# A transformer trunk in split fp32: the two matmuls of every wide block in one fixed order, the last block of a sum included

## The chip, the cores and the metric

One core of a Trainium2 chip. The metric is device time in microseconds (us) of one execution, the median of the runs; lower is better. TensorE (PE in the profile, its weight loads PEld) multiplies into PSUM, VectorE (DVE) and ScalarE (ACT) work on SBUF and PSUM, GpSimd (POOL) does little here, and SyncE (SP) issues the DMAs.

## The reference

Two layers on 256 latent tokens (and, in layer 0, on 256 context tokens that feed keys and values) of width 1024. Each layer has three sub-layers: SwiGLU, a mixer, SwiGLU, each behind an RMSNorm that is shifted and scaled per channel by a vector `m` worked out from the conditioning:

```python
def swiglu(h, w13, w2):
    a, b = jnp.split(h @ w13, 2, axis=-1)
    return (jax.nn.silu(a) * b) @ w2                 # 1024 -> 2*2816 -> 1024

def ffn_sublayer(h, m, g, w13, w2, base):
    hn = modulate(rms_norm(h, g), m[:, :, base], m[:, :, base + 1])
    return h + 0.5 * m[:, :, base + 2] * swiglu(hn, w13, w2)

for i in range(2):
    x = ffn_sublayer(x, ...)                         # the context too for i = 0
    x = x + m[5] * mixer_i(modulate(rms_norm(x)))    # i = 0: attention | pooling; i = 1: gated conv
    x = ffn_sublayer(x, ...)
return rms_norm(x, final_g)
```

All of it is fp32 with random weights.

## The kernel before

Activations lie transposed: channels on the 128 partitions, the 256 tokens along the free dimension. Each fp32 operand of a product is split in two parts in a narrower format, hi and lo, and a product is the sum of hi·hi, hi·lo and lo·hi. `mm3` does the three as three matmuls. Where an activation's two parts lie side by side as 512 columns, `mm2` needs two: the weights' hi part against all 512 columns (hi and lo at once, into columns 0 to 511 of a PSUM bank), and the weights' lo part against the 256 hi columns (into columns 0 to 255). This is a wide block; a sum is 8 blocks long over the 1024 channels, or 22 blocks long over the 2816 hidden units, all into one bank. An evacuation then adds the two halves of the bank: `joined` (ACT copies the upper half, DVE adds the lower) or `residual` (DVE adds the lower half, then the upper, to the residual stream `xl_all`).

Wide sums stand in five kinds of places, 148 sums in all: in three feed-forward sub-layers the hidden units f = 6 to 21 (`pf`, two sums each, 96), and the way back (`pz`, 8 sums of 22 blocks each, 24); the two output projections of the mixers (`pwo`, 8 and 8); the conv projections j = 4 to 7 (`pc` two sums, `pb` one, 12). The rest, from 0 to about 490 us and the first hidden units of each sub-layer, goes through `mm3` and a native fp32 form.

Weights come through `Stream`: SP loads 1 MB (`raw`, 3 buffers) with two chunks of 8 blocks in it; per chunk ACT casts the hi part (`whi`, line 102, 4 buffers) and DVE subtracts for the lo part (`wlo`, line 103, 4 buffers). A cast can start once PE has read the chunk four places earlier for the last time. DVE also works out the modulation vectors `m` (line 203, tile `jk`), doled out by `mod_credit`.

PSUM has three double banks (`pair`) and two single ones (`single`). `pf` and `pc` use pairs; `pz`, `pb` and most of `pwo` use singles, so sum d + 2 of these waits for the evacuation of sum d. In the output projections the first sums are begun without the block whose activation comes last (`early`), and that block is done afterwards (`rest`).

The order on each engine is fixed when the program is built: a scheduler with a cost of its own for each instruction places them, with priority for evacuations that feed the next sub-layer. So an edit in one place can reorder instructions elsewhere.

Of the kernel before, what the change touches and what calls it, by code (L numbers as in the profile page):

```python
# [119 lines left out]
def hybrid_trunk_kernel(ctx: ExitStack, tc: tile.TileContext, xc, cols_d, modw, wst, poolw_d,  # L120
                        rpb, notok_d, rcnt_d, out):
    nc = tc.nc
# [133 lines left out]
    def mm2(out, w, x, first, last):  # L256

        (wh, wl), both = w, x.rearrange("p a b -> p (a b)")
        if not last:
            nc.tensor.matmul(out, wh, both, start=first, stop=False)  # L260
        nc.tensor.matmul(out[:, 0:256], wl, x[:, 0, :], start=False, stop=False)  # L261
        if last:
            nc.tensor.matmul(out, wh, both, start=False, stop=True)  # L263

    class Rstd:

# [135 lines left out]
    def wide(pt, w, act):  # L402
        for k in range(KD):
            mm2(pt, (w[0][:, k, :], w[1][:, k, :]), act.op[:, k], k == 0, k == KD - 1)
# [493 lines left out]
    class OutProj:  # L898
# [7 lines left out]
        def block(self, d, k, first, last):  # L906
            assert (d, k) == self.order.pop(0)
            mm2(self.pts[d], W.block(), self.x[:, k], first, last)
# [27 lines left out]
    def ffn(act, l, s, gp, nxt_of, rate1, rate2):  # L936
# [44 lines left out]
        for d in range(KD):  # L981
            pt = single(f"pz{l}{s}{d}")
            for f in range(NF):
                if W.at_chunk():
                    mod_credit(rate2)
                mm2(pt, W.block(), g2[f], f == 0, f == NF - 1)
            residual(pt, d, l, s)
            nxt.feed(d)
# [214 lines left out]
```

## Time and profile before

| | |
|---|---|
| median of 3 runs | 1185.64 us (1185.47 to 1185.81) |
| profiled execution, its own time | 1185.92 us |
| its span, first to last instruction | 1184.1 us |
| mean granted TensorE clock | 0.990 of full speed |
| matmuls that end a wide sum (line 263) | 148 |

A group's row reads: line, engine, operation, tile written <- tiles read, shapes, count. In a row of the timeline the first number is the start in us from the span's start, the second the duration of the stretch; a matmul's duration includes its way through the array, and the next one starts before it ends, so the distance from start to start tells the pace. Equal rows that follow each other are merged ("x2").

### The profile page before, as it was taken

The numbers are of one execution on the slowest core, as the hardware profiler recorded it, in microseconds if no ns is written. First come the engines' busy times: TensorE is split into PE (matmuls) and PEld (weight loads), VectorE is DVE, ScalarE is ACT, GpSimd is POOL, SyncE is SP. The second block draws the span as 40 slices with busy tenths as digits, with TensorE's granted clock in tenths as the row PEclk, the third lists the DMA queues.
The fourth block names the chain that finished last, engine by engine and source line by source line (L and its number), as shares of the span: only waits on it lengthen the run. The fifth ranks groups of instructions, "written<-read, shape, count | busy, mean of one in ns | idle before, by whom it ended". The sixth has DMA issues, their size and how long they took to land.

```text
span 1184.1 us, 16775 instructions
## 1 busy us (share of the span) xinstructions
PE 1154.5 (97%) x6570; PEld 990.4 (84%) x6570; DVE 928.4 (78%) x1486; ACT 573.9 (48%) x890; POOL 21.1 (2%) x23
## 2 busy tenths in 40 slices
PE   4999999999999999999999999999999999999997
PEld 2568888888888987889888889888889989988886
DVE  8977686577788586788898998788998888766663
ACT  4353221223234445567556447555546656655642
POOL 2000000000000040000000000000000000000000
PEclk7999999999999999999999999999999999999998
DMA  7764455467676753245677985677895465555551
GB/s 274 255 221 156 179 191 185 143 217 275 241 272 238 230 136 90 76 165 187 242 264 271 342 316 205 221 271 260 314 336 188 149 213 174 183 181 191 198 179 36
DMA packets 45791, 250.54 MB, mean 212 GB/s; under 512 B 12944, under 2 KB 13328, under 8 KB 17552
## 3 DMA queue, kind: packets, MB, share of 16 engines
q1 hardware_dynamic: 45712, 249.48, 60.4%
q8 instruction: 51, 0.84, 0.3%
q14 instruction: 28, 0.23, 0.1%
HBM read 248.41 MB, written 1.05 MB: 211 GB/s over the span
## 4 chain that ended last, share of the span: by engine, by line
PE 93%; DVE 2%; DMA 1%; SPq 1%; ACT 1%; issue 1%; DVEq 0%; ACTq 0%
PE pf L260 13%; PE pz L260 10%; PE pf L261 8%; PE pa L253 6%; PE pa L254 6%; PE pa L252 6%; PE pz L261 5%; PE p L562 4%; PE py L253 3%; PE py L254 3%; PE py L252 3%; PE pf L253 3%; PE pf L252 3%; PE pf L254 3%; PE pwo L260 2%; PE pf L263 2%
## 5 line engine op out<-in xcount | busy, mean ns | idle before, releaser
L102 ACT CAST whi<-raw 128x1024 fp32r<-128x1024 f32 x312 | 327.8, 1051 | 394.2 <-PE pa L253 114.1
L103 DVE TENSOR_TENSOR wlo<-raw,whi 128x1024 fp32r<-128x1024 f32 x312 | 382.0, 1225 | 150.6 <-ACT whi L102 149.9
L260 PE MATMUL pf<-al,whi 128*128 128x512 f32 x672 | 241.0, 397 | 0.0
L203 DVE CUSTOM_DVE_ANT_0 jk<-mr,cvec,cols 128x1024 bf16<-128x1024 f32 x184 | 236.5, 1285 | 1.6
L261 PE MATMUL pf<-al,wlo 128*128 128x256 f32 x768 | 199.9, 281 | 0.0
L260 PE MATMUL pz<-g,whi 128*128 128x512 f32 x504 | 178.6, 398 | 0.0
L261 PEld LDWEIGHTS pf<-al,wlo 128*128 128x128 f32 x768 | 145.0, 189 | 8.9
L260 PEld LDWEIGHTS pf<-al,whi 128*128 128x128 f32 x672 | 126.4, 188 | 26.2
L261 PE MATMUL pz<-g,wlo 128*128 128x256 f32 x528 | 144.3, 281 | 0.0
L260 PEld LDWEIGHTS pz<-g,whi 128*128 128x128 f32 x504 | 94.7, 188 | 22.1
L252 PE MATMUL pa<-xh,whi 128*128 128x512 f32 x288 | 112.0, 389 | 0.0
L253 PE MATMUL pa<-xl,whi 128*128 128x512 f32 x288 | 112.0, 389 | 0.0
L254 PE MATMUL pa<-xh,wlo 128*128 128x512 f32 x288 | 112.0, 389 | 0.0
L261 PEld LDWEIGHTS pz<-g,wlo 128*128 128x128 f32 x528 | 99.7, 189 | 2.3
L253 PE MATMUL pf<-ah,whi 128*128 128x258 f32 x288 | 81.6, 283 | 0.0
L252 PE MATMUL pf<-ah,whi 128*128 128x258 f32 x288 | 80.9, 281 | 0.0
L254 PE MATMUL pf<-ah,wlo 128*128 128x258 f32 x288 | 80.8, 281 | 0.0
L252 PE MATMUL py<-gh,whi 128*128 128x512 f32 x176 | 68.5, 389 | 0.0
L253 PE MATMUL py<-gl,whi 128*128 128x512 f32 x176 | 68.5, 389 | 0.0
L254 PE MATMUL py<-gh,wlo 128*128 128x512 f32 x176 | 68.5, 389 | 0.0
L619 ACT COPY tf<-pf 128x512 f32<-128x512 f32 x48 | 28.2, 587 | 73.4 <-PE pf L263 73.4
L252 PEld LDWEIGHTS pa<-xh,whi 128*128 128x128 f32 x288 | 54.1, 188 | 11.3
(257 smaller groups left out, 1915.7 us busy)
## 6 DMA issues: line engine op xcount, KB each, us to landing
raw<-in_wst SPq DMA_DIRECT2D x156, 1024.0 KB, 5.0
mr<-in_modw SPq DMA_DIRECT2D x64, 1024.0 KB, 5.0
mr<-in_modw SPq DMA_DIRECT2D x16, 512.0 KB, 5.0
raw<-in_wst SPq DMA_DIRECT2D x8, 512.0 KB, 6.5
bias<-in_rpb SPq DMA_DIRECT2D x32, 64.0 KB, 5.8
xl_all<-in_xc SPq DMA_DIRECT2D x2, 512.0 KB, 6.7
xc_all<-in_xc SPq DMA_DIRECT2D x2, 512.0 KB, 8.1
out<-done SPq DMA_DIRECT2D x3, 256.0 KB, 2.6
```

The costliest lines, as they stand in the source:

```text
L102: nc.scalar.copy(hi, src)
L103: self.last = nc.vector.tensor_tensor(lo, src, hi.bitcast(F32), ALU.subtract).ins
L203: nc.vector.tensor_tensor_reduce(out=junk, in0=raw[:, h, :], in1=cvec[:, q, :], scale=1.0, scalar=cols[:, b : b + 1], op0=ALU.mult, op1=AL ...
L252: nc.tensor.matmul(out, wh, xh, start=first, stop=False)
L253: nc.tensor.matmul(out, wh, xl, start=False, stop=False)
L254: nc.tensor.matmul(out, wl, xh, start=False, stop=last)
L260: nc.tensor.matmul(out, wh, both, start=first, stop=False)
L261: nc.tensor.matmul(out[:, 0:256], wl, x[:, 0, :], start=False, stop=False)
L263: nc.tensor.matmul(out, wh, both, start=False, stop=True)
L562: nc.tensor.matmul(pts[j], wf[:, j * P : j * P + P], f32, start=first, stop=last)
L619: nc.scalar.copy(t, pt[:, :, 256:512])
```

## The change

In `mm2` the last block of a sum had its two matmuls in the other order: first the 256-column one, then the 512-column one, which closed the sum. Now every block has the 512-column matmul first and the 256-column one second, which closes the sum:

```diff
     def mm2(out, w, x, first, last):
 
         (wh, wl), both = w, x.rearrange("p a b -> p (a b)")
-        if not last:
-            nc.tensor.matmul(out, wh, both, start=first, stop=False)
-        nc.tensor.matmul(out[:, 0:256], wl, x[:, 0, :], start=False, stop=False)
-        if last:
-            nc.tensor.matmul(out, wh, both, start=False, stop=True)
+        nc.tensor.matmul(out, wh, both, start=first, stop=False)
+        nc.tensor.matmul(out[:, 0:256], wl, x[:, 0, :], start=False, stop=last)
```

Lines behind it move up by three: the 512-column matmul is line 259 in the kernel after, the 256-column one line 260, and line 619 becomes 616. Both kernels have 6450 matmuls of the same shapes. The upper half of the bank is final one matmul earlier than the lower now, so the built program lets the two be signalled apart: 729 instructions of PE signal to other engines instead of 623.

The end of a sum on PE, in a feed-forward sub-layer (`pf_5344` is the pair of f = 18, `pf_5395` of f = 19; `whi`, `wlo` with a number are a chunk of weights). Before:

```order
L260 MATMUL pf_5344<-al_4346,whi_5288 128x512
L261 MATMUL pf_5344<-al_4346,wlo_5289 128x256 x2
L263 MATMUL pf_5344<-al_4346,whi_5288 128x512
L260 MATMUL pf_5395<-al_4346,whi_5308 128x512
L261 MATMUL pf_5395<-al_4346,wlo_5309 128x256
L260 MATMUL pf_5395<-al_4346,whi_5308 128x512
```

And after:

```order
L259 MATMUL pf_5344<-al_4346,whi_5288 128x512
L260 MATMUL pf_5344<-al_4346,wlo_5289 128x256
L259 MATMUL pf_5344<-al_4346,whi_5288 128x512
L260 MATMUL pf_5344<-al_4346,wlo_5289 128x256
L259 MATMUL pf_5395<-al_4346,whi_5308 128x512
L260 MATMUL pf_5395<-al_4346,wlo_5309 128x256
```

The pair of 256-column matmuls and the pair of 512-column ones around a sum's end are gone; the two sizes alternate throughout.

ACT at the end of the first phase of layer 0's second feed-forward, f = 21 (`tf_5490` is the copy of `pf_5446`'s upper half, `sl_5489` its SiLU, `g_21_4204` the hidden unit that the last block of each `pz` sum reads). Before:

```order
L949 CAST g_20_4203<-sl_5438 128x256
L619 COPY tf_5490<-pf_5446 128x512
L102 CAST whi_5512<-raw_5345 128x1024
L947 ACTIVATE sl_5489<-tf_5490 128x256
L102 CAST whi_5539<-raw_5396 128x1024
L949 CAST g_21_4204<-sl_5489 128x256
L160 ACT_TABLE_LOAD
L160 ACTIVATE warm<-warm 128x1
L102 CAST whi_5561<-raw_5396 128x1024
```

And after:

```order
L946 CAST g_20_4203<-sl_5438 128x256
L102 CAST whi_5512<-raw_5345 128x1024
L616 COPY tf_5490<-pf_5446 128x512
L102 CAST whi_5539<-raw_5396 128x1024
L944 ACTIVATE sl_5489<-tf_5490 128x256
L102 CAST whi_5561<-raw_5396 128x1024
L946 CAST g_21_4204<-sl_5489 128x256
```

Each step of the evacuation now stands behind one more cast of weights. The same exchange of a cast and a copy stands at most f of the feed-forward sub-layers; on DVE the joins and the splits are exchanged likewise, and at this f two more `jk` and one more split stand ahead of `g_21_4204`.

PE at the end of the first `pz` sum of that sub-layer (`pz_5509`; `pz_5582` is the second). Before:

```order
L260 MATMUL pz_5509<-g_20_4203,whi_5469 128x512
L261 MATMUL pz_5509<-g_20_4203,wlo_5470 128x256
L261 MATMUL pz_5509<-g_21_4204,wlo_5470 128x256
L263 MATMUL pz_5509<-g_21_4204,whi_5469 128x512
L260 MATMUL pz_5582<-g_0_4183,whi_5469 128x512
```

And after:

```order
L259 MATMUL pz_5509<-g_20_4203,whi_5469 128x512
L260 MATMUL pz_5509<-g_20_4203,wlo_5470 128x256
L259 MATMUL pz_5582<-g_0_4183,whi_5469 128x512
L260 MATMUL pz_5582<-g_0_4183,wlo_5470 128x256
L259 MATMUL pz_5582<-g_1_4184,whi_5469 128x512
L260 MATMUL pz_5582<-g_1_4184,wlo_5470 128x256
L259 MATMUL pz_5582<-g_2_4185,whi_5512 128x512
L260 MATMUL pz_5582<-g_2_4185,wlo_5513 128x256
L259 MATMUL pz_5582<-g_3_4186,whi_5512 128x512
L259 MATMUL pz_5509<-g_21_4204,whi_5469 128x512
L260 MATMUL pz_5509<-g_21_4204,wlo_5470 128x256
```

Seven matmuls of the second sum now stand ahead of the first sum's last block. Two more places on PE are reordered: behind the even output projection nine matmuls of f = 1 move behind the rest of f = 0, and in the odd output projection five matmuls of the third sum (`pwo_8803`) move ahead of the second (`pwo_8784`), while on DVE the join `tb_8752`, which frees that second sum's bank, moves behind four instructions. On SP three loads change places.

## The prediction

> **What bounds the kernel now.** I read the page's busy times first, then the chain that ended last, then the busy time by stretches, and last the pace of single matmuls around the end of a sum, since the change sits there. The page's busy times and, from its section on the chain, the shares by engine:
>
> ```profile
> PE 1154.5 (97%) x6570; PEld 990.4 (84%) x6570; DVE 928.4 (78%) x1486; ACT 573.9 (48%) x890; POOL 21.1 (2%) x23
> PE 93%; DVE 2%; DMA 1%; SPq 1%; ACT 1%; issue 1%; DVEq 0%; ACTq 0%
> ```
>
> PE is busy 97% of the span and is 93% of the chain. These are averages, so the stretches in which wide sums run come next (busy us of PE, PEld, DVE, ACT, POOL, then the granted clock, the DMA share and GB/s):
>
> ```profile
> 527.00:644.50 117.50, 117.50 (x743) 105.77 (x742) 99.72 (x151) 73.67 (x116) 0.00 (x0) 1.00 0.67 236
> 644.50:709.00 64.50, 64.50 (x374) 56.35 (x373) 60.86 (x99) 32.20 (x42) 0.00 (x0) 1.00 0.88 320
> 963.00:990.00 27.00, 25.82 (x154) 22.46 (x153) 24.47 (x45) 16.69 (x27) 0.00 (x0) 1.00 0.47 167
> ```
>
> In layer 0's second feed-forward (527 to 644.5 the `pf` sums, 644.5 to 709 the `pz` sums) PE has no idle time at all and its clock is at full; DVE is at 99.72 of 117.50 and 60.86 of 64.50, close behind. So in these stretches only two things change the time: PE's own pace at the end of a sum, and something that DVE or ACT delivers late enough to stop PE. In the third stretch, around the odd output projection, PE is idle for 1.18 of 27.00 us; that wait is looked at below.
>
> **The pace at the end of a sum.** PE's rows at the end of one `pf` sum (start, duration; starts tell the pace):
>
> ```profile
> 600.09 0.40 PE L260 MATMUL pf<-al,whi 128*128 128x512 f32 x1
> ...
> 601.50 0.40 PE L260 MATMUL pf<-al,whi 128*128 128x512 f32 x1
> 601.74 0.40 PE L261 MATMUL pf<-al,wlo 128*128 128x256 f32 x2
> 601.98 0.40 PE L263 MATMUL pf<-al,whi 128*128 128x512 f32 x1
> 602.21 0.40 PE L260 MATMUL pf<-al,whi 128*128 128x512 f32 x1
> 602.45 0.28 PE L261 MATMUL pf<-al,wlo 128*128 128x256 f32 x1
> ```
>
> From 600.09 to 601.50 lie four alternating pairs of a 512- and a 256-column matmul: 1.41 us, .3525 a pair. Within a pair the 512 takes .24 (601.50 to 601.74). The two 256s at the boundary take 601.98 − 601.74 = .24, .12 each; the closing 512 takes 602.21 − 601.98 = .23, although it signals the evacuation, and the next sum's 512 takes .24. The two pairs across the boundary, 601.50 to 602.21, take .71 against 2 × .3525 = .705 inside. The same in a `pz` sum of 22 blocks:
>
> ```profile
> 644.51 0.40 PE L260 MATMUL pz<-g,whi 128*128 128x512 f32 x1
> ...
> 651.57 0.40 PE L260 MATMUL pz<-g,whi 128*128 128x512 f32 x1
> 651.80 0.40 PE L261 MATMUL pz<-g,wlo 128*128 128x256 f32 x2
> 652.04 0.40 PE L263 MATMUL pz<-g,whi 128*128 128x512 f32 x1
> 652.27 0.40 PE L260 MATMUL pz<-g,whi 128*128 128x512 f32 x1
> ```
>
> Twenty pairs from 644.51 to 651.57 are 7.06 us, .353 a pair; the two at the end, 651.57 to 652.27, are .70 against .706. So the order 512, 256, 256, 512 costs what 512, 256, 512, 256 costs, to about ±.01 us, which is the rounding of the rows: +.005 in one place, −.006 in the other.
>
> **The change part by part.**
>
> 1. *The exchange itself.* Nothing is removed or added on PE: 6450 matmuls of the same shapes. At each of 148 sums' ends two neighbours of equal size become two alternating pairs. By the rows above the gain is +.005 or −.006, and I take 0. The ends are ±.01 × 148 = ±1.5 us.
>
> 2. *The weight load that now follows a 256-column matmul.* At a boundary the next sum's first load ran beside a 512-column matmul (.23); now it runs beside a 256-column one (.12). That first load may also have to wait, for its chunk of weights or for its bank. The nearest row is the start of a chunk inside a sum, the ninth block of `pz`, whose load waits on ACT's cast and stands behind a 256. First PE, then the load:
>
> ```profile
> 647.21 0.28 PE L261 MATMUL pz<-g,wlo 128*128 128x256 f32 x1
> 647.33 0.40 PE L260 MATMUL pz<-g,whi 128*128 128x512 f32 x1
> ```
>
> ```profile
> 647.22 0.19 PEld L260 LDWEIGHTS pz<-g,whi 128*128 128x128 f32 x1
> ```
>
> The load begins with the 256 at 647.22 and lasts .19, yet the 512 starts .12 after the 256. So .12 of cover is enough, and I price this at 0. From below it is 0 (a load that is hidden already can't gain); the upper end, .19 − .12 = .07 a sum, is the first rival.
>
> 3. *Signals.* 106 more PE instructions signal. The closing 512, which signals today, takes .23, the plain one .24: 0, at most ±.01 × 106 = ±1.1 us, not in addition to the ±1.5, since it lies in the same boundary rows.
>
> 4. *The evacuation.* The upper half of the bank is final one matmul earlier and the lower half closes the sum. Time from a pair's start to the bank's end: before .12 + .40 = .52 (256 starts, 512 starts .12 later and lasts .40); now .24 + .28 = .52. So `joined`'s second step on DVE and the first step of `residual`, both of which read the lower half, start when they did. Only ACT's copy of the upper half may start earlier, by about .12 (.52 against .40). From the waits:
>
> ```profile
> ACT tf L619 <- PE pf L263: 73.4, 48, 1.8
> PE pwo L260 <- DVE xl_all L603: 2.4, 3, 1.1
> ```
>
> ACT waits for PE at 48 `pf` sums, 73.4 us in all: it has time to spare, and starting earlier hands nothing to PE, which waits for none of it. What covers this 0 is that the `g` tiles are read a whole phase later. The second row is PE's own wait, for `residual` to free the bank in the output projections; it hangs on the closing matmul and so stays. There the last block of each sum stands alone:
>
> ```profile
> 970.86 0.27 PE L261 MATMUL pwo<-y,wlo 128*128 128x256 f32 x1
> 970.98 0.40 PE L263 MATMUL pwo<-y,whi 128*128 128x512 f32 x1
> 972.49 0.47 PE L260 MATMUL pwo<-y,whi 128*128 128x512 f32 x1 [1.12 <-DVE xl_all L603]
> ```
>
> After it the 512 will start at about 970.86, the 256 at 971.10 and end at 971.38, as the 512 does now (970.98 + .40). The gap of 1.5 us to 972.49 remains: 0.
>
> 5. *Instructions that the scheduler moved.* Here a delivery can come late. The tightest is `g_21` at the end of layer 0's second feed-forward. DVE's and ACT's rows of before:
>
> ```profile
> 644.45 1.28 DVE L203 CUSTOM_DVE_ANT_0 jk<-mr,cvec,cols 128x1024 bf16<-128x1024 f32 x1
> 645.66 0.69 DVE L620 TENSOR_TENSOR tf<-pf,tf 128x512 f32<-128x512 f32 x1
> 646.26 1.28 DVE L203 CUSTOM_DVE_ANT_0 jk<-mr,cvec,cols 128x1024 bf16<-128x1024 f32 x1
> 647.46 0.42 DVE L948 TENSOR_TENSOR sl<-tf,sl 128x256 f32<-128x256 f32 x1
> 647.87 1.23 DVE L103 TENSOR_TENSOR wlo<-raw,whi 128x1024 fp32r<-128x1024 f32 x1
> 649.00 0.43 DVE L950 TENSOR_TENSOR g<-sl,g 128x256 fp32r<-128x256 f32 x1
> ```
>
> ```profile
> 648.37 0.40 ACT L949 CAST g<-sl 128x256 fp32r<-128x256 f32 x1
> 648.78 1.28 ACT L160 ACT_TABLE_LOAD   x1
> 650.29 1.05 ACT L102 CAST whi<-raw 128x1024 fp32r<-128x1024 f32 x1
> ```
>
> DVE now has two more `jk` (1.20 each, start to start) and one more split (1.13) ahead of `g_21`: 649.00 + 3.53 = 652.53, done by 652.96. ACT casts the hi part behind `whi_5561`, which starts no later than 650.29: 650.29 + 1.05 + .40 = 651.74, earlier than DVE. PE read `g_21` first at 651.80 + .12 = 651.92; seven matmuls now stand ahead of that, four 512s and three 256s, 4 × .235 + 3 × .12 = 1.30, so it is needed at 653.22. It is ready .26 early by the sum of durations; DVE's splits also wait for ACT's casts, which the sum leaves out, so I put the stall at 0 to .2 us.
>
> The odd output projection is the second place. `tb` frees the bank of the second sum:
>
> ```profile
> 963.35 0.42 DVE L620 TENSOR_TENSOR tb<-pb,tb 128x256 f32<-128x256 f32 x1
> 963.69 0.42 DVE L1013 TENSOR_TENSOR zpad<-tc 128x256 f32<-128x256 f32 x1
> ...
> 965.54 1.01 DVE L1016 SCALAR_TENSOR_TENSOR y<-zpad,cols,y 128x256 f32<-128x256 f32 x2
> ```
>
> ```profile
> 965.21 0.40 PE L260 MATMUL pwo<-y,whi 128*128 128x512 f32 x1
> ```
>
> Moved behind `zpad`, `y`, one split and the first of the two scalar-tensor operations, `tb` starts (965.54 − 963.69) + .52 = 2.37 later, at 965.72, and is done at 966.14. PE's first matmul of `pwo_8784` was at 965.21 and now stands behind three 512s and two 256s, .945: 966.15. A tie, 0 to .1 us. The third place, the nine `pf` matmuls that are exchanged behind the even projection, I give the bounds of the first, 0 to .2. Elsewhere a cast has changed places with a copy, on engines that DVE's 99.72 of 117.50 and ACT's 73.67 show to have room. The loads that change places on SP I price at 0: the DMA share is .67 there, and PE waited for nothing. Together 0 to .5, and I take .2.
>
> **The sum.** The profiled execution's own time is 1185.92 us (span 1184.1). 1185.92 + 0 (boundaries) + 0 (loads) + 0 (signals) + 0 (evacuation) + .2 (moved instructions) = 1186.1. The profiled execution stands .28 above the median of the runs, 1185.64, so against that median it is 1185.8.
>
> **The rivals.**
>
> *Slower, the load comes into the open.* If the next sum's first load can't begin until late in the last matmul, because it waits for a bank or a chunk, a 256 of .12 hides less of its .19 than a 512 of .23 did: up to .07 × 148 = 10.4 us, 1196. It decides from 2.4 / 148 = .016 us a sum. For it: each boundary does carry waits. Against it: the chunk start at 647.33, with a wait and the same cover, keeps the pace of .12. Chance .04.
>
> *Slower, the signals cost.* Were each of the 106 further signals to hold PE by what separates two rows, .01 us, it would be 1.1 us: 1186.9, still inside the bound of no change; to count, a signal would have to cost 2.4 / 106 = .023 us. The closing 512's .23 against .24 of one that doesn't signal speaks against any. Chance .04. The Trainium skill, "TensorE: Matmul & The Clock Gate", section "The cost: per-tile semaphore tail", speaks for this rival: increments on completion serialize, each adding about 26.3 ns to the tail of a group of tiles. By that figure the sum would be an estimated 106 × .0263 = 2.8 us more, 1188.6. The trace of before doesn't show it: the signalling matmul isn't followed by a longer step.
>
> *Slower, a moved delivery is late.* If at one of the three places a delivery slips by a whole split and `jk` (1.13 + 1.20), the stall is about 2.3 us, 1188.1. For it: DVE is at 60.86 of 64.50 us where `g_21` is made. Against it: the .26 left by the sum of durations. Chance .02.
>
> *Faster, a projection's wait goes.* If the earlier upper half let the bank free sooner, PE's 2.4 us of waits for `residual` at the projections would go: 1185.8 − 2.4 = 1183.4, or, with .005 less at each of the 96 `pf` boundaries, 1182.9. For it: the upper half is final sooner. Against it: `residual` reads the lower half first, which closes last. Chance .05.
>
> **How the numbers follow.** A measurement of this kernel can tell about 0.2%, 2.4 us, from no change; the three runs lie within .34 us. The likeliest is no change, .85, at 1185.8; faster .05; slower .04 + .04 + .02 = .10. The range comes from the bounds of the likeliest: ±1.5 for the boundaries, to which the moved instructions can add .3 above what I took; with the spread of the runs (.1) below, 1184.2 to 1187.7. The rivals outside it hold under .2.
>
> **What would show it right or wrong.** Right: PE's starts alternate by .24 and .12 straight through a sum's end, two `pf` sums are 16 × .3525 = 5.64 us apart, PE is busy in the whole of both stretches of the second feed-forward, and the wait at the odd projection is still about 1.1 us on `residual`. Wrong: a step of more than .13 behind each closing 256 (load or signals), idle time of PE on `g` in the first or second `pz` sum above .2 us or on `tb` at the odd projection, or a wait at the projections that is gone.

## The result, and the profile after

The kernel after takes 1180.59 us (median of 5 runs, 1179.86 to 1181.26) against 1185.71 for the kernel before in the same measurement: a ratio of .9948, 95% interval .9936 to .9959 (the two medians alone give .9957). Measured again later beside other kernels it took 1180.56 against 1185.79, .9956 (.9944 to .9969). The change makes the kernel faster by about 5.1 us, where no change was forecast (1184.2 to 1187.7).

The page of the kernel after, busy times and shares of the chain:

```profile
PE 1147.9 (97%) x6570; PEld 989.1 (84%) x6570; DVE 927.6 (79%) x1486; ACT 573.6 (49%) x890; POOL 21.1 (2%) x23
PE 93%; DVE 2%; DMA 1%; SPq 1%; ACT 1%; issue 1%; DVEq 0%; ACTq 0%
```

PE bounds it as before, with as many instructions; DVE and ACT do the same work, and PE's busy time fell by 6.6 us. So PE does the same matmuls faster. The clock doesn't explain it: its mean was .990 in the profiled execution before and .997 in the one after, but two runs of the kernel after at .990 took 1180.59 and 1179.86 us, and one of the kernel before at .997 took 1185.60. The stretches by busy time (the second one ends with the `pz` sums here, the last one is shifted with the kernel's progress):

```profile
527.00:644.50 117.50, 117.50 (x755) 107.00 (x755) 99.59 (x151) 74.06 (x117) 0.00 (x0) 1.00 0.69 243
644.50:705.70 61.20, 61.20 (x354) 53.47 (x353) 58.35 (x96) 30.97 (x41) 0.00 (x0) 1.00 0.91 328
959.50:986.50 27.00, 25.40 (x152) 22.03 (x151) 24.16 (x45) 16.71 (x27) 0.00 (x0) 1.00 0.49 170
```

In the first stretch PE has no idle time in either kernel, at a clock of 1.00 in both, but gets through 755 matmuls in 117.50 us instead of 743; at its end both kernels stand at the same place, the start of `pz` (644.51 and 644.57). The columns that one reads first, busy share and clock, show nothing; the count behind the "x" does. PE's rows around the first sum's end, with one far behind:

```profile
557.90 0.39 PE L259 MATMUL pf<-al,whi 128*128 128x512 f32 x1
...
558.25 0.39 PE L259 MATMUL pf<-al,whi 128*128 128x512 f32 x1
558.48 0.28 PE L260 MATMUL pf<-al,wlo 128*128 128x256 f32 x1
558.59 0.39 PE L259 MATMUL pf<-al,whi 128*128 128x512 f32 x1
558.82 0.28 PE L260 MATMUL pf<-al,wlo 128*128 128x256 f32 x1
558.94 0.39 PE L259 MATMUL pf<-al,whi 128*128 128x512 f32 x1
...
644.22 0.39 PE L259 MATMUL pf<-al,whi 128*128 128x512 f32 x1
```

The matmul at 558.48 ends a sum and signals; the next sum's starts .11 later. From 557.90 to 644.22 lie 249 pairs, .3467 us each. Before, a pair inside a sum took .3525. The gain lies in every pair, and not at the sums' ends. A group's mean shows it too, 397 ns for the 512-column matmuls of `pf` before and 391 after (first row before, second after):

```profile
L260 PE MATMUL pf<-al,whi 128*128 128x512 f32 x672 | 241.0, 397 | 0.0
```

```profile
L259 PE MATMUL pf<-al,whi 128*128 128x512 f32 x768 | 266.4, 391 | 0.0
```

Where the time went, by the start of the first matmul of each stage in the profiled executions (us; the stages left out differ by .13 at most between before and after). "Once", "pf only" and "twice, k = 6" are experiments of the next section:

| stage | before | after | after, again | once | pf only | twice, k = 6 |
|---|---|---|---|---|---|---|
| up to the even projection | 490.9 | 492.3 | 490.6 | 491.2 | 490.4 | 490.5 |
| even projection, first hidden units | 63.4 | 63.6 | 63.7 | 63.6 | 63.7 | 63.5 |
| `pf`, 256 pairs | 90.20 | 88.76 | 88.76 | 90.40 | 90.20 | 90.40 |
| `pz`, 176 pairs | 62.04 | 61.14 | 62.14 | 61.18 | 62.17 | 61.18 |
| layer 1: `pf` | 90.20 | 88.76 | 88.76 | 90.40 | 90.20 | 90.40 |
| `pz` | 62.04 | 61.01 | 61.01 | 62.19 | 62.17 | 62.19 |
| conv sums | 33.94 | 34.05 | 34.05 | 34.06 | 33.97 | 34.05 |
| odd projection | 18.25 | 18.65 | 18.79 | 18.79 | 18.14 | 18.79 |
| last: `pf` | 90.20 | 88.76 | 88.76 | 90.40 | 90.20 | 90.40 |
| `pz` | 62.04 | 61.01 | 61.01 | 62.19 | 62.18 | 62.19 |
| span | 1184.1 | 1178.7 | 1178.8 | 1185.3 | 1184.4 | 1184.7 |

From before to after, three `pf` stages give 3 x 1.44 = 4.32 us and three `pz` stages .90 + 1.03 + 1.03 = 2.96, together 7.28. In the second profile of the kernel after the first `pz` stage took 62.14, and the same sum is 6.28. The odd projection gives .40 back, the conv sums .11. The first row differs by 1.3 us and holds the same program in all kernels; over the profiles it lies between 490.3 and 492.3, and that is chance. 256 pairs in 88.76 us are .3467 each; 90.20 is .3523, and 90.40 .3531.

### The profile page after: what moved, and what is told of

Same layout as the page of the kernel before. It is cut to its first block, busy times and chain, and to the rows that moved or that the text cites. A ratio compares the mean times of both kernels' runs of the same rounds, so it can differ in the third digit from the quotient of the medians.

```text
span 1178.7 us, 16841 instructions
## 1 busy us (share of the span) xinstructions
PE 1147.9 (97%) x6570; PEld 989.1 (84%) x6570; DVE 927.6 (79%) x1486; ACT 573.6 (49%) x890; POOL 21.1 (2%) x23
## 4 chain that ended last, share of the span: by engine, by line
PE 93%; DVE 2%; DMA 1%; SPq 1%; ACT 1%; issue 1%; DVEq 0%; ACTq 0%
PE pf L259 15%; PE pz L259 10%; PE pf L260 8%; PE pa L254 6%; PE pa L253 6%; PE pa L252 6%; PE pz L260 5%; PE p L559 4%; PE py L254 3%; PE py L253 3%; PE py L252 3%; PE pf L253 3%; PE pf L252 3%; PE pf L254 3%; PE pwo L259 2%; PE pc L259 1%
## 5 line engine op out<-in xcount | busy, mean ns | idle before, releaser
L259 PE MATMUL pf<-al,whi 128*128 128x512 f32 x768 | 266.4, 391 | 0.0
L260 PE MATMUL pf<-al,wlo 128*128 128x256 f32 x768 | 215.1, 280 | 0.0
L259 PE MATMUL pz<-g,whi 128*128 128x512 f32 x528 | 183.2, 392 | 0.0
L259 PEld LDWEIGHTS pf<-al,whi 128*128 128x128 f32 x768 | 143.6, 187 | 31.4
L260 PE MATMUL pz<-g,wlo 128*128 128x256 f32 x528 | 147.2, 279 | 0.0
L259 PEld LDWEIGHTS pz<-g,whi 128*128 128x128 f32 x528 | 98.8, 187 | 22.1 <-DVE g L947 0.2
L253 PEld LDWEIGHTS pa<-xl,whi 128*128 128x128 f32 x288 | 54.1, 188 | 11.3
```

The source lines that it names most:

```text
L253: nc.tensor.matmul(out, wh, xl, start=False, stop=False)
```

## The experiments

Theory A after this reading: alternating 512- and 256-column matmuls have two paces that keep themselves up, .3467 and .3533 us a pair. Which one PE runs in depends on the phase in which the alternation began, and two equal neighbours (an exchange) set the phase anew. In the kernel before every sum's end did so, and mostly led to the slow pace; in the kernel after equal neighbours are left in three places alone, where the scheduler put blocks of one sum among those of another, and just one of them lies in the `pf` and `pz` stages (around `g_21` in layer 0's `pz`). The rivals: each sum's end costs something by itself (B), or the instructions that the scheduler moved on the other engines bring the gain (C).

**Three exchanges ("once").** The kernel after, and in the last block of three sums of 148 the old order:

```diff
-    def mm2(out, w, x, first, last):
+    def mm2(out, w, x, first, last, swap=False):
         (wh, wl), both = w, x.rearrange("p a b -> p (a b)")
-        nc.tensor.matmul(out, wh, both, start=first, stop=False)
-        nc.tensor.matmul(out[:, 0:256], wl, x[:, 0, :], start=False, stop=last)
+        if not swap:
+            nc.tensor.matmul(out, wh, both, start=first, stop=False)
+        nc.tensor.matmul(out[:, 0:256], wl, x[:, 0, :], start=False, stop=last and not swap)
+        if swap:
+            nc.tensor.matmul(out, wh, both, start=False, stop=last)
...
-                    wide(pt[:, h, :], w, act)
+                    wide(pt[:, h, :], w, act, KD - 1 if (f, h) == (F_RAW, 0) else None)
```

> The kernel after, with the old order (256, then 512) in the last block of three sums alone: the first wide pf sum (f = 6, a) of each of the three feed-forward sub-layers. The other 145 sums alternate; ACT, DVE and SP have the same instructions in the same order as in the kernel after. Theory A (a pair of equal neighbours on PE shifts its phase, and the pace of all alternating pairs behind it changes from .3467 to .3533 us a pair until something else interrupts PE): 272 + 2 x 423 pairs behind the three places, x .0067 = 7.4 us more than the kernel after, about 1188.0, slower even than before. Theory B (each sum's end costs by itself): three ends x .02 us = .06 us, about 1180.6. Theory C (the gain came from the moved instructions on ACT, DVE and SP): 1180.6 as well.

Measured: 1187.24 us (median of 11), a ratio to before of 1.0014 (1.0005 to 1.0023). The kernel before took 1185.98 in the same measurement: three exchanged pairs, at 3 of 148 sums' ends, cost the whole gain and 1.3 us more. PE's rows around the first of them:

```profile
555.53 0.39 PE L260 MATMUL pf<-al,whi 128*128 128x512 f32 x1
...
556.57 0.39 PE L260 MATMUL pf<-al,whi 128*128 128x512 f32 x1
...
557.15 0.40 PE L261 MATMUL pf<-al,wlo 128*128 128x256 f32 x2
557.38 0.40 PE L263 MATMUL pf<-al,whi 128*128 128x512 f32 x1
557.62 0.39 PE L260 MATMUL pf<-al,whi 128*128 128x512 f32 x1
...
557.96 0.40 PE L260 MATMUL pf<-al,whi 128*128 128x512 f32 x1
...
558.31 0.40 PE L260 MATMUL pf<-al,whi 128*128 128x512 f32 x1
...
558.67 0.40 PE L260 MATMUL pf<-al,whi 128*128 128x512 f32 x1
...
559.02 0.40 PE L260 MATMUL pf<-al,whi 128*128 128x512 f32 x1
...
560.08 0.40 PE L260 MATMUL pf<-al,whi 128*128 128x512 f32 x1
```

Ahead of the exchange three pairs take 1.04 us (.3467); behind it, from 557.96, six take 2.12 (.3533), and so it goes on: the same 87 us hold 495 matmuls before, 504 after, and 494 here (in this order).

```profile
557.00:644.00 87.00, 87.00 (x495) 75.63 (x494) 71.98 (x112) 50.03 (x78) 0.00 (x0) 1.00 0.72 256
```

```profile
557.00:644.00 87.00, 87.00 (x504) 76.71 (x503) 73.09 (x113) 50.46 (x79) 0.00 (x0) 1.00 0.73 256
```

```profile
557.00:644.00 87.00, 87.00 (x494) 75.51 (x493) 71.51 (x113) 50.17 (x78) 0.00 (x0) 1.00 0.72 255
```

Since ACT, DVE and SP run the same order as in the kernel after, B and C fall. The 272 + 2 x 423 slow pairs that theory A forecast are in the trace: against the kernel after, three `pf` stages of 90.40 and two `pz` stages of 62.19 add 3 x 1.64 + 2 x 1.18 = 7.28 us to the profiled execution. Its span is 6.5 longer and not 7.28, mainly because the table's first row was 1.1 shorter there.

**An exchange in the middle of each sum ("middle").** As above, with `swap` at k = 4 of 8, at f = 11 of 22, and at k = 4 of the sums of the projections that aren't begun early.

> The kernel after, with the two matmuls exchanged in one middle block (k = 4 of 8, f = 11 of 22) of each wide sum, the last block left as in the kernel after: equal neighbours inside each sum, where no bank changes, nothing is signalled and nothing is evacuated. Theory A (phase): most pairs run at .3533 us again, about as before: 1185 to 1188. Theory B (the end of a sum, where the bank changes and the evacuation is signalled): 1180.6. Theory C (moved instructions on the other engines): 1180.6.

Measured: 1187.20 us (median of 11), 1.0010 of before (1.0002 to 1.0019). `pf` takes 90.21 and `pz` 62.03 us, as before to a hundredth, although no bank changes and nothing is signalled where the exchange stands. The end of a sum isn't needed for it.

**The old order in `pf`, `pc` and `pb` alone ("pf only").** `swap` at k = 7 of 8 in `wide`.

> The old order in the last block of the pf, pc and pb sums (108 of 148), the new one in pz and pwo. Theory A (phase): the pf sums take 2.82 us again instead of 2.773, 96 x .047 = 4.5 us, the pz sums stay at 22 x .3467 = 7.63 us: about 1185.1. Theory C (moved instructions): ACT and DVE stand nearly as before, so all of the gain is gone: 1185.7.

Measured: 1187.07 us (median of 11), 1.0009 of before (1.0000 to 1.0018), and not 1185.1. The `pf` stages came back to 90.20 as expected. But the `pz` sums, whose order is that of the kernel after, took 62.17 instead of 61.0: they took over the slow pace in which the last `pf` exchange had left PE, and had no exchange of their own to leave it. That is theory A's own mechanism, which the expectation had not followed to its end.

**Matmuls alone ("bench").** Nothing but matmuls, from weights and activations that lie in SBUF; the rest of the computation is left out. The segments, with W for a 512- and w for a 256-column matmul:

```python
("warm", "Ww" * 120), ("alt", "Ww" * 66),
("sum22", ("Ww" * 21 + "wW") * 3), ("sum8", ("Ww" * 7 + "wW") * 8),
("kick", "Ww" * 21 + "wW" + "Ww" * 44),
("wide2", "Ww" * 22 + "W" + "Ww" * 44), ("narrow2", "Ww" * 22 + "w" + "Ww" * 44),
("mid22", ("Ww" * 11 + "wW" + "Ww" * 10) * 3), ("mid8", ("Ww" * 4 + "wW" + "Ww" * 3) * 8),
("group8", ("W" * 8 + "w" * 8) * 8), ("group2", "WWww" * 33), ("wide", "W" * 60), ("narrow", "w" * 60)
```

> Only matmuls of the two sizes, in segments of 60 to 132, each into one bank; weights and activations lie in SBUF, no transfers run. First with ACT and DVE idle, then with ACT casting and DVE subtracting 128x1024 tiles beside it. Segments: alternating; alternating with the two matmuls exchanged once (kick), at the end of every 8 or 22 blocks (sum8, sum22), in the middle of every 8 or 22 blocks (mid8, mid22); with one extra 512 or one extra 256 (wide2, narrow2); eight 512s and then eight 256s (group8); two and two (group2). Theory A (phase): alternating pairs take .347 us, and .353 behind an exchange, with ACT and DVE idle as well. Theory B (sum ends): .347 everywhere, since no bank changes. Theory D (the slow pace comes of PE's and ACT's or DVE's accesses meeting): .353 in the second half alone. By A the groups of eight, with few changes of size, take no more than alternating pairs: .345 to .347 a pair.

The first two segments, ACT and DVE idle, each with two 512-column matmuls that lie 60 pairs apart:

```profile
25.31 0.39 PE L182 MATMUL warm_alone<-x,wh 128*128 128x512 f32 x1
...
46.11 0.39 PE L182 MATMUL warm_alone<-x,wh 128*128 128x512 f32 x1
...
58.01 0.40 PE L182 MATMUL alt_alone<-x,wh 128*128 128x512 f32 x1
...
79.21 0.40 PE L182 MATMUL alt_alone<-x,wh 128*128 128x512 f32 x1
```

20.80 us against 21.20: .3467 and .3533 a pair, from the same instructions, with no exchange in either. Behind PE's idle time the pace comes out either way, so "alternating is fast" (expected by A) is wrong as it stands: alternating keeps the pace that it has. With ACT and DVE busy the roles came out the other way round (warm .353, alt .347), so their traffic isn't needed for the slow pace (theory D falls). 512s alone step by 226.7 ns and 256s alone by 120.0; the fast pace is exactly their sum. Groups of eight 512s and eight 256s take 349 ns a pair every time, between the two paces, and not .345 to .347.

**Leaving the slow pace again ("twice").** In the slow pace the pairs repeat in threes, 361, 349 and 350 ns (the trace keeps starts to the ns; in the rows of "once" above, from 557.96 on, the first three are .35, .36, .35); the next pace hangs on which of the three stands ahead of an exchange. Counted over the traces of before, "once", "middle", "pf only" and the two runs here, wherever five whole pairs without a wait of PE stand on both sides of an exchange:

| ahead of the exchange | behind it slow | behind it fast |
|---|---|---|
| the 361 | 180 | 0 |
| the 349 | 161 | 0 |
| the 350 | 0 | 11 |
| the fast pace | 26 | 0 |

Blocks of eight (a sum of `pf`) never brought an exchange behind the 350, which is why the `pf` sums of before stayed slow.

The matmuls alone of "bench" and "widths" (below), counted likewise, add 4 of 4 to the fast pace behind the 350 and 0 of 35 behind the other two, but out of the fast pace 5 of 6 only: the sixth (the first exchange of "sum22" with ACT and DVE busy) left a fast pace of another form, 350 and 343 ns in turn, and the pace stayed fast. The 26 of the table all left the even form, 346 to 347 ns a pair. A single extra 512 or 256 ("wide2", "narrow2") changed the pace in one case of four, from slow to fast behind an extra 256.

To try the rule, each feed-forward got a second exchange, in block 5 or in block 6 of the next sum:

```diff
-                    wide(pt[:, h, :], w, act, KD - 1 if (f, h) == (F_RAW, 0) else None)
+                    wide(pt[:, h, :], w, act, {(F_RAW, 0): KD - 1, (F_RAW, 1): 5}.get((f, h)))
```

> As the run with three exchanges, and one exchange more in each feed-forward sub-layer: block k = 5 of the next sum (f = 6, b). In that run the pairs of this sum take 344, 350, 361, 349, 350, 361, 349, 350 ns. In all traces so far an exchange right behind the second pair after a 361 (the one of 350 that follows the 349) was followed by the fast pace, one behind the 361 or behind the 349 by the slow pace. Block 5 follows such a 350. Theory A with this rule (the phase decides): PE goes back to .3467 a pair, about the kernel after, 1180.6. Rival (each exchange only adds, or the slow pace stays until PE stands still): 1187.2.

> The same with the second exchange one block later, k = 6, right behind the 361. Theory A with the rule: the slow pace stays, 1187.2. Rival (any second exchange undoes the first): 1180.6.

Measured: 1180.42 us with k = 5 (.9955 of before, .9942 to .9967) and 1187.44 with k = 6 (1.0015, 1.0006 to 1.0025). One block's place decides 7 us. Stretches of 82 us in two sub-layers, k = 5 and then k = 6:

```profile
560.00:642.00 82.00, 82.00 (x475) 72.28 (x474) 69.65 (x109) 48.38 (x76) 0.00 (x0) 1.00 0.72 260
746.00:828.00 82.00, 82.00 (x475) 72.28 (x474) 68.91 (x100) 47.82 (x74) 0.00 (x0) 1.00 0.74 262
```

```profile
560.00:642.00 82.00, 82.00 (x467) 71.08 (x466) 68.64 (x108) 47.47 (x75) 0.00 (x0) 1.00 0.72 259
746.00:828.00 82.00, 82.00 (x466) 71.08 (x465) 67.34 (x99) 46.89 (x72) 0.00 (x0) 1.00 0.72 257
```

**A try at a faster version ("fixed").** `swap` in block 3 of the second `pc` sum alone, to lead the conv sums out of the slow pace.

> The kernel after with one exchange, in block k = 3 of the second pc sum (j = 4). In the kernel after the conv projections run at the slow pace from the third conv pair behind a wait of PE at 929 us on: 447, 350, 361, 349, 350, 361 ns, and block 3 of this sum follows a 350 that follows a 349. By the rule the 90 pairs behind it go at .3467: .6 us less than the kernel after, if that wait of PE ends at the same phase again; if it doesn't, the exchange does nothing or ends the fast pace, 0 to .7 us more. No difference that the times alone would tell; the pairs in the trace tell it.

Measured: 1181.07 us (1178.60 to 1182.06), no difference from the kernel after. PE's wait at the conv sums ended at another phase (the pairs behind it read 447, 463, 345, 350, 360 and not 448, 447, 350, 361), so block 3 followed the pair behind the 360, and the slow pace stayed, as the rule has it for that place. An exchange placed by the rule behind a wait of PE hits its place only if the wait ends at the same phase.

**The kernel after once more.**

> The kernel after once more, beside the three others on the same chip: 1180 to 1181.5. Whether the pace in its wide stages comes out the same again: theory A expects .3467 in all three feed-forward sub-layers, since each is entered from the same sequence of matmuls.

Measured: 1180.56 us (1180.23 to 1181.15). The three `pf` stages and two `pz` stages are the same to a hundredth. In layer 0's `pz` the slow pace ran (62.14 for 61.14): there PE waits for `g_21`, and the moved block sets two 512s and then two 256s side by side; the pace behind differs from run to run. In "once" PE doesn't wait at this place, and the pace turned from slow to fast there (61.18), so the neighbours can do it alone; what the wait adds isn't separated.

**Other widths ("widths").** Matmuls alone, 512 columns alternating with other widths and an exchange every 10 to 12 pairs:

> Only matmuls again, ACT and DVE idle: 512 columns alternating with a narrower one of 128, 192, 224, 240, 248, 256, 258, 264, 272, 288, 320, 384 or 448 columns, 12 segments' worth of pairs with an exchange after 12, 10, 11, 12, 10, 11 and 12 pairs, so that different phases are met; and 40 of the narrow ones alone. So far the steps of 512 alone are 226.7 ns, of 256 alone 120.0, and a pair takes 346.7, their sum, or 353.3. Theory L (the slow pace comes of the next weight load, which starts 3 to 5 ns behind the matmul before it and takes about as long as a matmul of 256 columns): two paces for widths about 256 and below, one pace, the sum of the two steps, for 320 and more. Theory S (a rounding of each step to a grid of 6.67 ns, whatever the load does): two paces at most widths, 6.67 ns apart, the wide ones included.

Steps of the narrow one alone, the sum with 226.7, and a pair (the mean of the last six pairs ahead of each exchange, median over the stretches; two numbers where there are two paces), in ns:

| columns | 128 | 192 | 240 | 256 | 258 | 288 | 320 | 384 | 448 |
|---|---|---|---|---|---|---|---|---|---|
| alone | 111.7 | 111.7 | 112.1 | 120.0 | 120.7 | 131.7 | 146.7 | 173.3 | 202.7 |
| sum | 338.4 | 338.4 | 338.8 | 346.7 | 347.4 | 358.4 | 373.4 | 400.0 | 429.4 |
| pair | 340.0 | 340.0 or 344.5 | 340.0 | 346.7 or 353.3 | 353.6 | 363.3 or 364.4 | 379.9 | 406.7 or 413.3 | 437.8 |

Of the four widths that the table leaves out, 224, 248 and 264 columns showed one pace each (343.3, 346.7 and 350.0), and 272 two (357.3 or 360.0).

Neither theory holds. Two paces are not a matter of the weight load as theory L had it, since 384 has them too (L falls; the loads last .19 us, a 256-column matmul .28 at steps of .12), and most widths showed one pace only, off the sum by anything from 1 to 13 ns (S falls as it stands). Something of S's grid may be there, though: 340.0, 346.7, 353.3, 360.0, 406.7 and 413.3 are whole multiples of 6.67 ns, and 343.3, 350.0 and 363.3 lie halfway between two, while the others do neither; the runs don't say why. What sets the pace within PE stays open; that it comes out fast or slow without any other engine, transfer, signal or bank change is shown by the matmuls alone.

## Why the prediction was wrong

*What bounds the kernel*: right. PE bounds it, and its pace decides.

*Step 1, the exchange itself*: this failed. It took 0, with ends of ±.01 us at each of 148 sums' ends, ±1.5 us; measured were 7.28 us in the wide stages of the profiled execution (6.28 in the second profile), 5.1 in the time of the whole kernel. The working compared the two pairs across a boundary with the pairs inside a sum, .705, and took that inner .3525 as given. But .3525 was itself a consequence of the order at the last boundary. The unit of cost was the sum's end; it should have been every alternating pair, 1296 of them in the table's `pf` and `pz` stages (3 x 432), at up to .0067 us. The trace of before held the sign: its second `pz` sum runs from 652.27, quoted in the prediction, to

```profile
659.91 0.39 PE L260 MATMUL pz<-g,whi 128*128 128x512 f32 x1
```

7.64 us for 22 blocks, .3473 each, against 7.76 from 644.51 to 652.27 for the first. Two equal sums, both without idle time, differ by .12 us: twelve times the bound that was taken. One more sum laid beside the one that was read would have shown that the pace isn't a constant. None of the prediction's signs of being wrong came up, since all of them look at one place; of its signs of being right two failed, the distance of two `pf` sums, which is 16 x .3467 = 5.55 us and not 5.64, and the wait of step 4.

Part of the gain is luck. `pf` is entered in the fast pace in every profile here, and the unbroken order keeps it; "once" shows that the unbroken order keeps a slow pace as well, at 90.40 us a stage instead of the 90.20 of before. Why the entry is fast isn't shown.

*Step 2, the weight load*: right. The closing 256 is followed by the next sum's 512 after .11 to .12 (558.48 to 558.59).

*Step 3, signals*: right. 106 more signals, and the matmul that signals is followed at the same pace. The estimate of 2.8 us, which the prediction worked out from the Trainium skill ("TensorE: Matmul & The Clock Gate", section "The cost: per-tile semaphore tail"), doesn't agree with this trace: the last `pf` stage has the signals of 32 sums and its pairs take .3467, the bare sum of the two steps.

*Step 4, the evacuation*: right that PE's wait in the odd projection stays. But it grew, to 1.60 us from 1.12 (after, then "pf only"):

```profile
967.90 0.28 PE L260 MATMUL pwo<-y,wlo 128*128 128x256 f32 x1
969.78 0.47 PE L259 MATMUL pwo<-y,whi 128*128 128x512 f32 x1 [1.60 <-DVE xl_all L600]
```

```profile
972.60 0.47 PE L260 MATMUL pwo<-y,whi 128*128 128x512 f32 x1 [1.11 <-DVE xl_all L603]
```

It lies between 1.60 and 1.68 in all seven runs with the moved instructions. "pf only", where the projections' blocks have the new order but the other engines stand nearly as before, has 1.11: the half microsecond belongs to step 5, not to the evacuation.

*Step 5, moved instructions*: right for `g_21`, too small for the odd projection, where 0 to .1 was taken and the stage grew by .40. `g_21` was put at a stall of 0 to .2. DVE and PE of the kernel after:

```profile
652.66 0.41 DVE L947 TENSOR_TENSOR g<-sl,g 128x256 fp32r<-128x256 f32 x1
```

```profile
652.88 0.74 PE L259 MATMUL pz<-g,whi 128*128 128x512 f32 x2
653.47 0.40 PE L260 MATMUL pz<-g,wlo 128*128 128x256 f32 x2
```

`g_21` is done at 653.07, and the two 512s take .59 from 652.88 to 653.47 where they'd take .46: a stall of .13. What the working didn't see is that the phase is set anew at this place, by the wait or by the equal neighbours that the moved block brings: 149 pairs behind it ran fast in one profile and slow in another, 1.0 us.

*The rivals*: none named the mechanism. "Faster, a projection's wait goes" had the right side with .05, for a wait that did not go.

## What to carry to other kernels

A pace read from a trace, even over hundreds of steps, is that of the state which the order before it has set; ahead of pricing an edit in a dense stream of matmuls, compare several equal stretches of the trace, and if they differ without idle time, the stream has more than one pace and the edit can switch between them. Where matmuls of two sizes alternate and are entered in the fast pace, as here, keep the alternation unbroken over sums and banks; and look at matmuls per us in stretches without idle time, since busy share and clock don't show the difference. A gain of this kind hangs on phase: a single exchange can take it away, and what comes behind a wait can differ from run to run.

## What the runs showed of the hardware

Matmuls of 512 and 256 columns that alternate run at 346.7 ns a pair, the sum of the steps of each alone (226.7 and 120.0), or at 353.3, in a pattern of three pairs (361, 349, 350) that holds for 423 pairs; the pace is kept until an exchange or a wait, and comes out either way from the same instructions. In the kernels an exchange led out of the slow pace only right behind the pair of 350 (11 of 11, against 0 of 341 behind the other two), and out of the even form of the fast pace always (26 of 26); a fast pace of 350 and 343 ns in turn outlasted the one exchange that it met. Alternating 512 with 258 columns took 353.6 ns for a sum of 347.4, with 384 columns 406.7 or 413.3 for a sum of 400.0.
